# Seven products of a Strassen-Winograd feed-forward in another order, x reloaded in two halves, and modulation sums held back in the mixer

## The chip, the cores and the metric

The kernel runs on one core of a Trainium2 chip. The core has TensorE (PE, whose weight loads the profile lists apart as PEld), VectorE (DVE), ScalarE (ACT), GpSimd (POOL) and SyncE (SP), which here does nothing but issue transfers, in order. The metric is the time of one execution on the device, in microseconds; smaller is better. The kernel before has a median of 1758.36 us over three runs (1758.32 to 1759.86).

## The reference

One layer of an autoregressive trunk on 1024 tokens of width 1024, in float32:

```
x <- x + 1/2 * g1 * SwiGLU_1( adaLN_1(RMSNorm(x)) )
h  = adaLN_2(RMSNorm(x));  [b, c, v, u] = split(h @ W_in)
   yA = b * conv3_causal(c * v)                    (512 channels)
   yB = GLU( Re(C . state) + D*u ),  state_t = Abar state_(t-1) + Bbar u_t   (512 channels)
x <- x + g2 * ( [RMSNorm(yA) | RMSNorm(yB)] @ W_out )
x <- x + 1/2 * g3 * SwiGLU_2( adaLN_3(RMSNorm(x)) )
y  = RMSNorm_final(x)
swiglu(h) = (silu(h @ w_gate) * (h @ w_up)) @ w_down
```

Shift, scale and gate of every sub-layer are columns of silu(cond) @ W_mod + b_mod; they are called the modulation vectors below. The hidden width of a feed-forward is 2816.

## The kernel before, in words

**Arithmetic.** A float32 operand is split into a rounded high part and the rest, and every product is three matmuls: high by high, high by rest, rest by high (`mm3`). So one weight granule has to be loaded, copied to its high part by ACT and subtracted to its rest by VectorE (`Weights.pump`, the groups `w<-raw`). Each call of `mm3` is one tick of a clock that the program keeps while it is written (`Clock.tick`); every `period` ticks the clock takes one step of the side work that is queued, so `clock.period` sets how thinly side work is strewn among the matmuls. The Tile scheduler then sets the final order of each engine's instructions.

**Stages.** The first feed-forward has eleven groups of hidden columns, fa0 to fa10. fa0 to fa3 are plain. From fa4 on each group goes through `seven`: for gate (side g) and then up (side u) the 2 x 2 block product is made of seven products in place of eight, by Winograd's scheme. A product is four calls of `mm3`, twelve matmuls on 128x512. The left blocks A11, A12, A22 and sums S1 to S4 of the normalized activations are made once; the weight blocks' sums t1 to t4 are made for every group by GpSimd (`Weights.combine`, lines L163 and L164; `split_done`, L172 for t2 and L174 for t4). `Weights.SEVEN` is the order in which the weight chunks are prepared: 0, t2, 3, t3, t1, t4, 2. t2 is written over chunk 0 once that is split; t4 = chunk 3 - t2 is written over chunk 3 once that is split, so that both adds stand inside a granule, between what ACT copies.

**Banks of sums.** The list `SEVEN` ahead of `seven` names for each product its left block and its PSUM bank: A11 in A, S2 in B, A12 in A on top of A11, S3 in D, S1 in C, A22 in E, S4 in C. Between them come the additions that take the results out:

```
A.copy(t1[:], bank["A"][:])      # n == 0
add(u2, t1, "B")                 # n == 1
add(u3, u2, "D")                 # n == 3
add(t1, u3, "C")                 # n == 4
add(u3, u3, "E")                 # n == 5
add(u2, u2, "C")                 # n == 6
```

u3 shows in the profile under the name of its tile, fa7gt, fa7gu and so on (a group, a side, a tile). S1's sum has to be out of bank C before S4's first matmul opens it again: in the order before, A22's product is all that stands between. There are six banks for these (`mm_ps`), handed round.

**Around them.** While fa4 to fa9 run, `side1` puts the tables of the S5 state space on VectorE (tiles rot, rott, bb, bl, cl), one step every 7 ticks. The products' results are kept in DRAM (`keep`). `down7` does the down product with the same seven products over chunks of four groups, called fad0 and fad1, each in two passes p = 0 and 1; its left blocks are fetched again (`fetch_chunk`, the names fa1lA, fa1lS) and its weights are raw tiles loaded from in_ds. x, which had to give up its room, is loaded again from DRAM at the start of fa10 by eight transfers of 512 KB (`load_x`).

The mixer follows (w_in, the S5 part, conv, the gated unit `glu`, `w_out`). `side2` makes the modulation vectors of the second feed-forward in it: 24 loads of 512 KB into two buffers (tile wm) and for each a sum on VectorE. In `glu` the root of the norm's mean square is worked out on VectorE by a chain of small operations (nBanv, nBani, nBana, nBany, nBarb), and PE spreads nBarb over the partitions into nBabc. The second feed-forward has the groups fb0 to fb10: fb0 plain, fb1 to fb10 through `seven`, and between fb1's products the down product of fb0, called fb0d (`between` in `seven`, behind the product at position `place`, 0 for fb1).

## Time and profile before

| what | value |
|---|---|
| median of three runs | 1758.36 us |
| the profiled execution | 1760.56 us |
| its span | 1758.8 us |
| PE busy | 1681.3 us, 96% |
| VectorE busy | 1307.3 us, 74% |
| ACT, POOL busy | 569.1 us, 351.2 us |
| mean granted clock of PE | 0.986 |
| read from and written to HBM | 212.47 MB, 86.51 MB |

The span is the stretch from the first to the last instruction that the profiler recorded; the execution's own time has 1.8 us around it. Busy times are by engine and overlap. A row of the waits names who waited for which operation of which engine, for how long in all, how often, and the longest. In a timeline the number in brackets is the idle time of the engine just before, with what ended it.

### The profile page before, as it was taken

Reading aid. Unit: us, or ns where it says so; the run is one execution under the profiler, and the core shown is the slowest. Engines: PE = TensorE matmul, PEld = TensorE weight load, DVE = VectorE, ACT = ScalarE, POOL = GpSimd, SP = SyncE. Lnnn points to the kernel's source line nnn. Section 1 sums busy time; section 2 is a strip of 40 time slices with the busy share of each in tenths; the row PEclk is TensorE's granted clock in tenths of the full one; section 3 lists DMA queues with packets and bytes.
Section 4 is the critical chain, followed back from the end, with each engine's and each line's share of the span. In section 5 each row is a group of like instructions: output and inputs, shape, how many; then the busy total and the mean of one; then the engine's idle time right before and its main releaser. Section 6 shows DMA issues by size and latency. Waiting matters only on the chain.

```text
span 1758.8 us, 20854 instructions
## 1 busy us (share of the span) xinstructions
PE 1681.3 (96%) x7532; PEld 1381.2 (79%) x7532; DVE 1307.3 (74%) x2286; ACT 569.1 (32%) x934; POOL 351.2 (20%) x241
## 2 busy tenths in 40 slices
PE   4999999988999999999999899999999999999996
PEld 3788877876887888878887678878888888888886
DVE  7999899989666687553566876986777666677656
ACT  4223234433332221232213423433344443322221
POOL 0000032232232221100000021023322322333311
PEclk9999999999999999999999999999999999999998
DMA  8245544444677968215664451014344434669312
GB/s 322 80 148 193 203 158 172 171 160 171 230 304 289 355 222 301 88 59 161 191 191 120 149 199 36 25 50 166 132 155 171 166 132 155 226 252 358 120 48 96
DMA packets 101081, 304.55 MB, mean 173 GB/s; under 512 B 19057, under 2 KB 34673, under 8 KB 89842
## 3 DMA queue, kind: packets, MB, share of 16 engines
q1 hardware_dynamic: 100978, 303.22, 47.9%
q8 instruction: 59, 0.97, 0.2%
q14 instruction: 44, 0.36, 0.1%
HBM read 212.47 MB, written 86.51 MB: 170 GB/s over the span
## 4 chain that ended last, share of the span: by engine, by line
PE 63%; DVE 8%; DMA 3%; issue 1%; POOL 1%; ACT 1%; SPq 0%; DVEq 0%; POOLq 0%; ACTq 0%
PE wo L107 4%; PE fald L107 3%; PE fb10d L107 2%; PE u L107 2%; PE fbd_1B L107 2%; PE fbd_0B L107 2%; PE fad_1B L107 2%; DVE w L107 2%; PE fad_0B L107 2%; PE v L107 1%; PE b L107 1%; DMA swz<-si 1%; PE c L107 1%; DVE x L107 1%; PE fb0g L107 1%; PE fbd_1C L107 1%
## 5 line engine op out<-in xcount | busy, mean ns | idle before, releaser
L107 ACT CAST w<-raw 128x512 fp32r<-128x512 f32 (+1 forms) x358 | 237.4, 689 | 527.6 <-POOL raw L172 122.5
L107 DVE TENSOR_TENSOR w<-raw,w 128x512 fp32r<-128x512 f32 (+1 forms) x358 | 303.0, 863 | 136.3 <-ACT w L107 134.9
L172 POOL TENSOR_TENSOR raw<-sums,raw 128x512 f32<-128x512 f32 x50 | 78.0, 1560 | 414.0 <-DVE w L107 387.7
L163 POOL TENSOR_TENSOR sums<-raw 128x512 f32<-128x512 f32 x50 | 69.1, 1382 | 408.6 <-DMA raw<-in_gs 234.1
L174 POOL TENSOR_TENSOR raw<-raw 128x512 f32<-128x512 f32 x50 | 79.8, 1597 | 104.2 <-DVE w L107 95.9
L107 DVE CUSTOM_DVE_ANT_0 wm<-wm,cact 128x1024 f32<-128x1024 f32 x56 | 77.8, 1398 | 14.3 <-DMA wm<-in_wmod 14.2
L164 POOL TENSOR_TENSOR raw<-raw 128x512 f32<-128x512 f32 x50 | 76.5, 1529 | 3.9
L364 POOL TENSOR_TENSOR n3aq<-n3aq,n3aq 128x512 f32<-128x512 f32 x5 | 8.4, 1671 | 283.0 <-DMA wm<-in_wmod 257.4
L107 DVE TENSOR_TENSOR w<-sums,w 128x512 fp32r<-128x512 f32 x50 | 61.7, 1246 | 3.7 <-ACT w L107 3.4
L107 PE MATMUL p<-h,w 128*128 128x512 f32 x192 | 49.6, 421 | 8.1 <-DVE h L107 5.3
L107 PEld LDWEIGHTS p<-h,w 128*128 128x128 f32 x192 | 39.1, 205 | 18.6 <-DVE h L107 6.6
L107 PE MATMUL wo<-oa,w 128*128 128x512 f32 x192 | 45.7, 392 | 1.9 <-ACT w L107 1.2
L107 PE MATMUL v<-h,w 128*128 128x512 f32 x192 | 46.8, 395 | 0.0
L107 PE MATMUL c<-h,w 128*128 128x512 f32 x192 | 46.6, 394 | 0.0
L107 PE MATMUL u<-h,w 128*128 128x512 f32 x192 | 46.3, 401 | 0.2 <-DVE h L107 0.2
L107 PE MATMUL b<-h,w 128*128 128x512 f32 x192 | 45.6, 393 | 0.0
L107 PE MATMUL wo<-ob,w 128*128 128x512 f32 x192 | 45.2, 391 | 0.0
L107 PEld LDWEIGHTS wo<-oa,w 128*128 128x128 f32 x192 | 35.8, 188 | 10.1 <-ACT w L107 1.6
L107 PEld LDWEIGHTS u<-h,w 128*128 128x128 f32 x192 | 36.8, 194 | 8.7 <-DVE h L107 0.6
L107 PEld LDWEIGHTS wo<-ob,w 128*128 128x128 f32 x192 | 35.8, 188 | 7.4
L107 PEld LDWEIGHTS b<-h,w 128*128 128x128 f32 x192 | 35.5, 188 | 7.2
L107 PEld LDWEIGHTS c<-h,w 128*128 128x128 f32 x192 | 35.4, 188 | 7.0
(1565 smaller groups left out, 4042.0 us busy)
## 6 DMA issues: line engine op xcount, KB each, us to landing
raw<-in_gs SPq DMA_DIRECT2D x34, 1024.0 KB, 5.2
wm<-in_wmod SPq DMA_DIRECT2D x56, 512.0 KB, 5.2
raw<-in_ds SPq DMA_DIRECT2D x16, 1024.0 KB, 7.1
raw<-in_gu SPq DMA_DIRECT2D x10, 1024.0 KB, 8.1
mw<-in_wm SPq DMA_DIRECT2D x8, 1024.0 KB, 12.6
x<-in_x SPq DMA_DIRECT2D x16, 512.0 KB, 6.7
raw<-in_win SPq DMA_DIRECT2D x8, 1024.0 KB, 5.6
raw<-in_wl SPq DMA_DIRECT2D x5, 1024.0 KB, 5.5
```

The lines of the kernel that those rows point to most:

```text
L107: r = getattr(self.engine, name)(*args, **kw)
L163: self.G.tensor_tensor(out=f, in0=r[2], in1=r[1], op=ALU.subtract)
L164: self.G.tensor_tensor(out=r[1], in0=r[1], in1=r[0], op=ALU.subtract)
L172: self.G.tensor_tensor(out=r, in0=s["t3"], in1=r, op=ALU.add)
L174: self.G.tensor_tensor(out=r, in0=r, in1=s["t2"], op=ALU.subtract)
L364: nc.gpsimd.tensor_tensor(out=a, in0=a, in1=sq[:, :n], op=ALU.add)
```

## The change

There are three edits.

1. **The order of the seven.** For gate and up the products now go A11, S1, S2, S3, A12, A22, S4, in the banks A, C, B, D, A, E, C. S1's sum is taken out behind S3's, in one go with u3, so that A12's and A22's products stand between it and S4's. The evacuation of A12's bank moves behind the fifth product. The weight chunks go 0, t1, t2, t3, 3, t4, 2; t4 is now written over t2, as soon as that is split, a granule ahead of its use. The tile of the first quarter, c11, comes from another pool where the special one is closed. The down products keep the order of before, as `SECOND`. The callbacks are given a block's name in place of its number. The period of the side work goes from 7 to 7.75.
2. **x in two halves.** At the start of fa10 four of the eight loads are called, the tiles 0 and 2 of both token halves; tiles 1 and 3 are called in the first pass of fad0, behind its third product.
3. **The mixer's sums.** The period for side2 goes from 10 to 8 ahead of the gated unit, is 1000 from there until five tasks of the output product have been called, and 3 after them (before, it was 5 behind the second half of the gated unit).

How the instructions move is seen in the order in which the engines hold them. TensorE in the middle of fa7's gate side, before (fa7gC is bank C of group fa7, side g; h1S are the activations' sums, h_1 the second token half; x3 are the three matmuls of a split product):

```order
L107 MATMUL fa7gC<-h1S_3_1670,w_3259 128x512 x3
L107 MATMUL fa7gE<-h_1_419,w_3259 128x512 x3
L107 MATMUL fa7gE<-h_1_458,w_3259 128x512 x3
L107 MATMUL fa7gE<-h_1_497,w_3259 128x512 x3
L107 MATMUL fa7gE<-h_1_531,w_3259 128x512 x3
L107 MATMUL fa7gC<-h1S_0_2073,w_3314 128x512 x3
```

and with the change:

```order
L107 MATMUL fa7gD<-h1S_3_1708,w_3161 128x512 x3
L107 MATMUL fa7gA<-h_0_416,w_3225 128x512 x3
L107 MATMUL fa7gA<-h_0_455,w_3225 128x512 x3
L107 MATMUL fa7gA<-h_0_494,w_3225 128x512 x3
L107 MATMUL fa7gA<-h_0_528,w_3225 128x512 x3
L107 MATMUL fa7gE<-h_1_419,w_3225 128x512 x3
L107 MATMUL fa7gE<-h_1_458,w_3225 128x512 x3
L107 MATMUL fa7gE<-h_1_497,w_3225 128x512 x3
L107 MATMUL fa7gE<-h_1_531,w_3225 128x512 x3
L107 MATMUL fa7gC<-h1S_0_2073,w_3263 128x512 x3
```

The four rows of fa7gE alone stood between the two uses of fa7gC; now the rows of fa7gA stand ahead of them too, and the first use of C lies further up, behind A11's rows.

SP around the end of fa10, before (kept10A is a result of fa10 that goes to DRAM and waits for it; raw are the weights of the second pass of fad0):

```order
L107 DMA fa1lS_4638<-kept1S_545 128x1024
L107 DMA kept10A_600<-fa10A_4627 128x1024
L107 DMA fa2lS_4640<-kept2S_552 128x1024
L107 DMA fa3lS_4642<-kept3S_559 128x1024
L107 DMA fa4lS_4644<-kept4S_566 128x1024
L107 DMA raw_4780<-in_ds 128x2048
L107 DMA raw_4812<-in_ds 128x2048
```

and with the change:

```order
L107 DMA kept10A_600<-fa10A_4625 128x1024
L107 DMA fa1lS_4634<-kept1S_545 128x1024
L107 DMA fa2lS_4636<-kept2S_552 128x1024
L107 DMA fa3lS_4638<-kept3S_559 128x1024
L107 DMA fa4lS_4640<-kept4S_566 128x1024
L107 DMA x_1_4306<-in_x 128x1024
L107 DMA raw_4780<-in_ds 128x2048
L107 DMA raw_4812<-in_ds 128x2048
```

The fetch fa1lS went from ahead of kept10A to behind it, and the last load of x stands ahead of the two raw loads; seven others of x go earlier, as all eight did.

VectorE in the gated unit, before (wm ... scl is a sum of side2, into the scale):

```order
L107 ISA wm_3_0_7957,scl<-wm_3_0_7957,cact_7580 128x1024
L107 ISA scl 128x1
L107 TENSOR_SCALAR nBani<-nBani 128x4
L107 TENSOR_TENSOR nBana<-nBani 128x4
L107 SCALAR_TENSOR_TENSOR nBana<-nBana,nBanv 128x4
L107 ISA wm_3_1_7996,scl<-wm_3_1_7996,cact_7580 128x1024
L107 ISA scl 128x1
L107 SCALAR_TENSOR_TENSOR nBany<-nBana,nBani 128x4
L107 TENSOR_TENSOR scl<-scl,cols 128x8
L107 TENSOR_TENSOR nBana<-nBany 128x4
L107 SCALAR_TENSOR_TENSOR scl<-scl,cols 128x8
L107 SCALAR_TENSOR_TENSOR nBana<-nBana,nBanv 128x4
```

and with the change, up to nBarb:

```order
L107 SCALAR_TENSOR_TENSOR nBana<-nBana,nBanv 128x4
L107 SCALAR_TENSOR_TENSOR nBany<-nBana,nBani 128x4
L107 TENSOR_TENSOR nBana<-nBany 128x4
L107 SCALAR_TENSOR_TENSOR nBana<-nBana,nBanv 128x4
L107 SCALAR_TENSOR_TENSOR nBany<-nBana,nBany 128x4
L107 TENSOR_TENSOR nBana<-nBany 128x4
L107 SCALAR_TENSOR_TENSOR nBana<-nBana,nBanv 128x4
L107 ISA wm_3_0_8289,scl<-wm_3_0_8289,cact_7580 128x1024
L107 ISA scl 128x1
L107 SCALAR_TENSOR_TENSOR nBany<-nBana,nBany 128x4
L107 COPY nBarb<-nBany 128x512
L107 TENSOR_TENSOR yb_7573<-yb_7573,gs_1_8018 128x512
```

The scheduler has put other sums at this place: before, wm_3_0 and wm_3_1 stood between nBani and nBarb, and wm_2_0 and wm_2_1 ahead of nBanv; now it is wm_2_0 and wm_2_1 (a few rows further up) and wm_3_0, and wm_3_1 stands behind.

The diff:

```diff
--- before.py
+++ after.py
 class Weights:
-    SEVEN = (0, "t2", 3, "t3", "t1", "t4", 2)
+    SEVEN = (0, "t1", "t2", "t3", 3, "t4", 2)
+    SECOND = (0, "t2", 3, "t3", "t1", "t4", 2)
     def __init__(self, engines, srcs, granules, raw_bufs):
...
         self.G.tensor_tensor(out=r[1], in0=r[1], in1=r[0], op=ALU.subtract)
-        self.sums[j] = {"t1": r[1], "t2": r[0], "t3": f, "t4": r[3]}
+        self.sums[j] = {"t1": r[1], "t2": r[0], "t3": f, "t4": r[0]}
     def split_done(self, j, c):
-        if j in self.combined and c in (0, 3):
-            s, r = self.sums[j], self.chunk(j, c)
+        if j in self.combined and c in (0, "t2"):
+            s, r = self.sums[j], self.raws[j][:, :HALF]
             if c == 0:
...
             else:
-                self.G.tensor_tensor(out=r, in0=r, in1=s["t2"], op=ALU.subtract)
+                self.G.tensor_tensor(out=r, in0=self.chunk(j, 3), in1=r, op=ALU.subtract)
     def chunk(self, j, c):
...
                 srcs.extend([ds[c, p, 0], ds[c, p, 1]])
-                granules.extend([(j, s), (j + 1, s)] for s in Weights.SEVEN)
+                granules.extend([(j, s), (j + 1, s)] for s in Weights.SECOND)
         plain([wl[i] for i in range(wl.shape[0])])
...
                     x[2 * k + i][h] = xt[k][h][:, i, :]
-    def load_x(h):
-        for k in range(KT // 2):
-            SP.dma_start(xt[k][h][:], x_d[h, :, 2 * k : 2 * k + 2, :])
+    def load_x(hs, ks=range(KT // 2)):
+        for h in hs:
+            for k in ks:
+                SP.dma_start(xt[k][h][:], x_d[h, :, 2 * k : 2 * k + 2, :])
     def mm3(out, w, k, act, first, last, tok=slice(0, HALF), more=False):
...
             yield
-    SEVEN = (("A11", "A"), ("S2", "B"), ("A12", "A"), ("S3", "D"), ("S1", "C"), ("A22", "E"), ("S4", "C"))
+    SEVEN = (("A11", "A"), ("S1", "C"), ("S2", "B"), ("S3", "D"), ("A12", "A"), ("A22", "E"), ("S4", "C"))
+    SECOND = (("A11", "A"), ("S2", "B"), ("A12", "A"), ("S3", "B"), ("S1", "C"), ("A22", "B"), ("S4", "C"))
     def seven(name, between, place=1, kept=None, then=None):
...
                     A.copy(t1[:], bank["A"][:])
-                elif n == 1:
+                elif n == 2:
                     u2 = t2k(nm + "u2")
                     add(u2, t1, "B")
-                elif n == 2 and side == "g":
-                    t = pools["first"].tile([P, HALF], F32, tag="first", name=nm + "c11") if "first" in pools else t2k(nm + "c11")
+                elif n == 3:
+                    u3 = t2k(nm + "u3")
+                    add(u3, u2, "D")
+                    add(t1, u3, "C")
+                    out(1, 1, t1)
+                elif n == 4 and side == "g":
+                    t = pools["first"].tile([P, HALF], F32, tag="first", name=nm + "c11") if "first" in pools else acc_in_mov(nm + "c11")
                     A.activation(t[:], bank["A"][:], AF.Silu)
                     gate_[0, 0] = t
-                elif n == 2:
+                elif n == 4:
                     t = gate_[0, 0]
...
                         keep(kept, "A11", t, name)
-                elif n == 3:
-                    u3 = t2k(nm + "u3")
-                    add(u3, u2, "D")
-                elif n == 4:
-                    add(t1, u3, "C")
-                    out(1, 1, t1)
                 elif n == 5:
...
                         keep_sums(kept, gate_[0, 0], u3, t1, name)
-                else:
+                elif n == 6:
                     add(u2, u2, "C")
...
                 if side == "u" and then is not None:
-                    then(n)
+                    then(left)
         return a_tiles
...
         return t[:, 0, :], t[:, 1, :]
-    def down7(name, lefts, n_, then=None):
+    def down7(name, lefts, n_, then=None, first=None):
         for p in range(2):
...
                 V.tensor_tensor(out=dst[i][:], in0=src[i][:], in1=bank[b, i][:], op=ALU.add)
-            for n, (left, b) in enumerate(SEVEN):
+            for n, (left, b) in enumerate(SECOND):
                 (w,) = ws.take()
-                b = "B" if b in "DE" else b
                 for i in range(2):
...
                 ws.free()
-                if p and then is not None:
-                    then(n)
+                if (first, then)[p] is not None:
+                    (first, then)[p](left)
     def down2(a_tiles, n, name, halves=(1, 0)):
...
     mod_load(0)
-    load_x(0)
-    load_x(1)
+    load_x(range(2))
     ws.load(1)
...
         gate_up(act1, f"fa{g}", kept[g], g == SEVEN_FROM[0] - 1)
-    clock.period = 7
+    clock.period = 7.75
     lefts = [{left: [] for left, _ in SEVEN} for _ in range(CHUNKS)]
...
     HOMES = dict(A11="A", S2="B", A12="A", S3="B", S1="B", A22="A", S4="A")
-    def fetch_chunk(c, n, name="fa"):
-        left = SEVEN[n][0]
+    def fetch_chunk(c, left, name="fa"):
         for g in range(1 + 4 * c, 5 + 4 * c):
             lefts[c][left].append(fetch(kept[g], left, HOMES[left], f"{name}{g}l"))
-    def fetch_last(n):
-        if n in (0, 2, 5):
-            i = (0, 2, 5).index(n)
+    def fetch_last(left):
+        if left in ("A11", "A12", "A22"):
+            i = ("A11", "A12", "A22").index(left)
             for h in range(2):
...
             open_x(ctx)
-            for h in range(2):
-                load_x(h)
+            load_x(range(2), (0, 2))
         if g == NGRP - 2:
             pools.pop("first")
-        seven(f"fa{g}", lambda: None, kept=kept[g], then=(lambda n: fetch_chunk(0, n)) if g == NGRP - 1 else None)
-    down7("fad0", lefts[0], 0, lambda n: fetch_chunk(1, n))
+        seven(f"fa{g}", lambda: None, kept=kept[g], then=(lambda left: fetch_chunk(0, left)) if g == NGRP - 1 else None)
+    down7("fad0", lefts[0], 0, lambda left: fetch_chunk(1, left), lambda left: load_x(range(2), (1, 3)) if left == "A12" else None)
     clock.period = 8
...
     SP.dma_start(pools["cact"][:], cact_d[:])
-    clock.period = 10
+    clock.period = 8
     clock.side.append(side2(lambda name: wmp.tile([P, 1024], F32, tag="wm", name=name, bufs=2)[:], (SC3, SH3, G3)))
...
             n3[h].add(x[d][h], beside=d < 6)
+    clock.period = 1000
     wgl = ws.take(2)
...
     glu(1)
-    clock.period = 5
     ws.free(2)
...
     w_out((0, 1), 1, 1)
+    clock.period = 3
     ws.free(2)
...
     a_last = {}
-    def fetch_last(n):
-        if n == 0:
+    def fetch_last(left):
+        if left == "A11":
             for h in range(2):
...
         seven(f"fb{g}", lambda: None, kept=kept[g])
-    a_prev = seven("fb10", lambda: None, then=lambda n: fetch_chunk(0, n, "fb"))
-    down7("fbd0", lefts[0], 2, lambda n: fetch_chunk(1, n, "fb"))
+    a_prev = seven("fb10", lambda: None, then=lambda left: fetch_chunk(0, left, "fb"))
+    down7("fbd0", lefts[0], 2, lambda left: fetch_chunk(1, left, "fb"))
     down7("fbd1", lefts[1], 2, fetch_last)
```

## The prediction

> **What bounds the kernel now.** I read the head of the page first. The groups of costly instructions name VectorE and ACT, but the share of the span belongs to TensorE:
>
> ```profile
> span 1758.8 us, 20854 instructions
> PE 1681.3 (96%) x7532; PEld 1381.2 (79%) x7532; DVE 1307.3 (74%) x2286; ACT 569.1 (32%) x934; POOL 351.2 (20%) x241
> ```
>
> PE is idle for 1758.8 − 1681.3 = 77.5 us in all, prologue and tail included. The change takes no matmul away, so it can win only idle time of PE and time at a low clock. Next, the windows over the stage that the new order touches most, the first feed-forward's groups fa4 to fa9 (columns: stretch, its length, busy us of PE, PEld, DVE, ACT and POOL with counts, granted clock, DMA share, GB/s):
>
> ```profile
> 240.00:280.00 40.00, 36.88 (x160) 29.41 (x159) 39.02 (x64) 14.82 (x26) 9.23 (x7) 0.96 0.50 175
> 280.00:320.00 40.00, 38.25 (x174) 31.08 (x173) 36.98 (x58) 16.44 (x29) 11.50 (x8) 1.00 0.44 164
> 320.00:360.00 40.00, 39.74 (x181) 32.28 (x181) 37.28 (x62) 15.31 (x27) 11.97 (x8) 1.00 0.44 163
> 360.00:400.00 40.00, 34.71 (x149) 27.32 (x147) 33.12 (x50) 12.98 (x23) 12.78 (x8) 0.96 0.40 132
> 400.00:440.00 40.00, 34.63 (x150) 27.37 (x150) 36.14 (x58) 13.62 (x25) 13.16 (x8) 0.96 0.48 175
> 440.00:480.00 40.00, 40.00 (x175) 32.59 (x174) 25.52 (x42) 16.06 (x28) 10.20 (x8) 0.95 0.61 221
> sum 240.00, PE 224.21 PEld 180.06 DVE 208.06 ACT 89.23 POOL 68.83; mean PE 37.37 PEld 30.01 DVE 34.68 ACT 14.87 POOL 11.47
> 235.60:436.90 201.30, 186.36 (x822) 149.27 (x821) 181.97 (x287) 74.32 (x131) 60.73 (x38) 0.98 0.46 164
> ```
>
> PE lacks 240 − 224.2 = 15.8 us here. What the clock withholds is 40 × (0.04 + 0 + 0 + 0.04 + 0.04 + 0.05) = 6.8 us. So **22.6 us are in play**. While the side work on the S5 tables runs, VectorE is the fuller engine; in 440–480, without it, PE lacks nothing. The waits of PE, VectorE and ACT in 240–480 (total, times, longest, us) name the hand-over:
>
> ```profile
> PE fa7gC L107 <- DVE fa7gt L107: 4.6, 1, 4.6
> PE fa8uC L107 <- DVE fa8ut L107: 3.8, 1, 3.8
> PE fa4uC L107 <- DVE fa4ut L107: 2.4, 1, 2.4
> PE fa5gC L107 <- DVE fa5gt L107: 1.8, 1, 1.8
> PE fa8uA L107 <- ACT fa8ut L107: 1.1, 1, 1.1
> DVE w L107 <- ACT w L107: 17.6, 11, 3.2
> ACT w L107 <- POOL raw L172: 22.2, 8, 4.6
> ```
>
> Bank C holds S1's product, VectorE adds it out, and S4's product opens C again. The timeline of fa7g shows it, with E's product the only cover between:
>
> ```profile
> 358.83 2.85 POOL L172 TENSOR_TENSOR raw<-sums,raw 128x512 f32<-128x512 f32 x1 [14.81 <-DVE w L107]
> 360.90 2.88 PE L107 MATMUL fa7gE<-h,w 128*128 128x512 f32 x12
> 361.72 1.14 ACT L107 CAST w<-raw 128x512 fp32r<-128x512 f32 x2 [4.26 <-POOL raw L172]
> 364.19 1.75 DVE L107 TENSOR_TENSOR rot<-rs,rt 128x512 f32<-128x512 f32 x1
> 368.34 4.57 PE L107 MATMUL fa7gC<-h1S,w 128*128 128x512 f32 x12 [4.56 <-DVE fa7gt L107]
> 371.01 0.68 DVE L107 TENSOR_TENSOR rot<-rs,rt 128x512 f32<-128x512 f32 x1
> 458.77 2.72 PE fa9gE L107 x12
> ```
>
> The last row is from the chain of waits: twelve matmuls of one product take 2.72 us when nothing holds them. The twelve after the stall took 4.57 us, at a clock that had dropped.
>
> **Edit 1, the seven products.** Between S1's sum out of C and S4's product there is one product now, 2.72 us; afterwards there are two (A12, A22), 5.44. A12 waits for A11's copy behind three products, not one, so the 1.1-us kind of wait goes. VectorE must keep pace too. The busy time per instruction in fa4u to fa8u is 181.97 / 287 = 0.634 us. I counted VectorE's instructions in the two orders between successive last C sums, side by side (4u, 5g, … 8u): before 30, 37, 22, 38, 21, 42, 29, 32, 35; after 28, 28, 32, 27, 31, 39, 20, 39, 21. The sum goes from 286 to 265, or 182 to 168 us, because the period of 7.75 pushes side work into fa9: 9g goes from 28 to 40 and 9u from 13 to 21. PE itself needs about 201.3 − 15 of stalls − 4 of clock = 182 us for these nine, so VectorE falls below PE in the sum; the peaks remain. One side is 7 × 2.72 = 19.0 us of PE. At 7g VectorE needs 39 × 0.634 = 24.7, an excess of 5.7, and 6u before it (31 × 0.634 = 19.7) leaves 0.6 more; the cover is 5.44 − 0.69 for the sum itself = 4.75. So 7g still stalls 0.6 + 5.7 − 4.75 = 1.5, 8g 0.9 and 9g (25.4) 1.6: 4.0 us, and I add 1 for one half-length low-clock stretch. The term is 5 − 22.6 = **−17.6**. Bounds: −22.6 (all vanishes) and −6 (VectorE stays the bound, below).
>
> The clock deserves a look: a gap of 2.44 us in fa4u, and the clock behind it (the same columns as above):
>
> ```profile
> 259.41 4.57 PE L107 MATMUL fa4uC<-h1S,w 128*128 128x512 f32 x12 [2.44 <-DVE fa4ut L107]
> 260.00:264.00 4.00, 4.00 (x13) 3.14 (x12) 3.96 (x5) 0.62 (x1) 1.62 (x1) 0.63 0.17 66
> ```
>
> The 2.44-us gap brought 0.63. [...]
>
> **Edit 1's weights.** t2 and t4 are made a granule earlier, so ACT no longer queues behind POOL within a granule: the 22.2 us of ACT and, through it, much of VectorE's 17.6. The POOL adds then run beside a VectorE that works. The rows speak of a price: `rot` took 1.75 us beside POOL's 2.85-us add and 0.68 alone. [...] The result that this gives is the second rival. The same POOL and ACT instructions run either way; −17.6 holds their move at nothing, covered by VectorE's 182 − 168 = 14 us of new room.
>
> **Edit 2, x in two halves.** Of the eight 512-KB loads, the first four stay where all eight were, at the start of fa10, and three of the rest still go early. On SP's in-order queue the fourth, and the fetch fa1lS, which stood ahead of kept10A, now stand behind kept10A and ahead of the two raw loads for down7's second half. These rows show that place:
>
> ```profile
> 545.71 0.32 SPq L107 DMA_DIRECT2D kept10A<-fa10A  x1
> 547.89 0.87 SPq L107 DMA_DIRECT2D raw<-in_ds  x2
> 553.00:557.00 4.00, 4.00 (x20) 3.30 (x19) 1.71 (x3) 0.39 (x1) 0.36 (x1) 1.00 1.02 430
> 556.64 1.29 POOL L163 TENSOR_TENSOR sums<-raw 128x512 f32<-128x512 f32 x1 [28.93 <-DMA raw<-in_ds]
> PE fad_0A L107 <- DVE w L107: 3.2, 3, 1.9
> 566.00:570.00 4.00, 3.80 (x10) 3.00 (x11) 2.18 (x3) 0.99 (x2) 3.92 (x3) 0.59 0.03 12
> ```
>
> POOL waits for the raws, and PE, behind POOL, ACT and VectorE, already stalls 3.2 us; nothing covers more. Two more transfers of 0.52 MB at 430 GB/s are **+2.4 us**. Bounds: −4.8 (the stall, and 4 × 0.41 = 1.6 of clock, go because x leaves the link early) and +4.5 (twice the delay less an overlap of its issue). The first half of x: nothing, under fa10's matmuls.
>
> **Edit 3, the gated unit.** These rows carry it, the last showing the length of one sum:
>
> ```profile
> PE nBabc L107 <- DVE nBarb L107: 4.9, 1, 4.9
> 988.00:1020.00 32.00, 27.09 (x125) 22.47 (x123) 29.02 (x68) 13.03 (x20) 2.34 (x1) 0.95 0.47 161
> 993.38 1.22 DVE L107 CUSTOM_DVE_ANT_0 wm<-wm,cact 128x1024 f32<-128x1024 f32 x1
> ```
>
> The period of 1000 lets no new sum start there, yet in the new order the scheduler still leaves three in VectorE's chain up to nBarb: the count ahead of it falls by one only, 1.22 us, and wm_3_0 now needs a load that can go only after wm_2_0 is added. I take **−0.5**, bounds −6.5 (4.9 and 32 × 0.05 of clock) and +2. The sums held back follow in w_out, where VectorE has room until 1100; I take 0, ±1.
>
> **Edit 1 in the second feed-forward.** From fb2 on VectorE has no side work, and nothing changes. At fb1, A12 was second, and PE used it between fb0's down products:
>
> ```profile
> 1160.22 1.98 PE L107 MATMUL fb1gA<-h,w 128*128 128x512 f32 x8
> PE fb0d L107 <- DVE x L107: 1.7, 3, 0.7
> ```
>
> In the new order nothing stands there: 0 to +2.7 (one product), and I take **+1.5**.
>
> **The sum** is −17.6 + 2.4 − 0.5 + 1.5 = −14.2. The profiled execution took 1760.6 (1758.8 in its span and 1.8 around it), 2.2 above the median of the runs, 1758.36. So 1746.4 for such an execution and **1744.2** for the median.
>
> **Rivals.**
> 1. *All cover holds.* E's and A12's products hide every peak (−22.6), the raws come no later (0), and the chain in the gated unit empties (−4.9): 1758.4 − 27.5 + 1.5 = 1732. For it: the waits outside 7g and 8u are 2.4 us and less, under the new 2.72 of cover. Against it: three peaks of 39 and 40 instructions.
> 2. *VectorE stays the bound.* POOL's adds, which ran in VectorE's 17.6 idle us, now block it: while they overlap it does 0.68 / 1.75 = 0.39 of its work, so 17.6 × 0.61 = 10.7 us more. With all of its 19.3 idle us kept it needs 168 + 10.7 + 19.3 = 198 of 201.3 (−3.3); with half, 188 (−13). Midway −8, and with the other terms −4.6: 1754. For it: the `rot` rows. Against it: PE stood still in 360–440 while VectorE was idle too, so its room was unused.
> 3. *Slower, by bank B.* Bank C is now second in a side and B third, so if banks go round in turn the next side's S2 takes the bank that S4's sum has to free: two products after S4, 5.44 us, where it was five, 13.6. Should VectorE come over 4.75 us late to S4's sum, PE waits in every side; at 6.4 late (two weight chunks behind ACT's 3.2) it is (6.4 + 0.69 − 5.44) × 12 = 20 us: 1764. Against it, this sum in fa4u started 1.6 us after S4's last product (259.41 + 4.57 = 263.98), and in fb1g it waited for PE:
>
> ```profile
> 265.46 0.68 DVE L107 TENSOR_TENSOR fa4uu<-fa4uu,fa4uC 128x512 f32<-128x512 f32 x1
> 1180.80 0.69 DVE L107 TENSOR_TENSOR fb1gu<-fb1gu,fb1gC 128x512 f32<-128x512 f32 x1 [0.36 <-PE fb1gC L107]
> ```
> 4. *The change doesn't do what it says, the other way round:* I hold that the sums stay in the gated unit. If they do leave it, the 4.9-us wait goes, not 0.5: 1740.
>
> **How the numbers follow.** Forecast 0.56, by itself 1738 to 1750 (term 1 by ±4, the rest by ±2). Rival 1: 0.12; rival 2: 0.2; rival 3: 0.06; rival 4: 0.06. The measurement can tell about 0.2%, 3.5 us, from no change. Faster: 0.56 + 0.12 + 0.06 and half of rival 2's 0.2, 0.84; same: the other half, 0.1; slower 0.06. The range 1733 to 1756 leaves out rival 3, the lower half of rival 1 and the ends of 2 and of the forecast, about 0.18.
>
> **What would show it.** Right: PE's waits on fa4 to fa8 sums at some 4 us, all in front of 7g, 8g and 9g; ACT's wait for POOL under 5 us; clock 0.99 and more in these windows; fad_0A's wait at 5 to 6; nBabc's at 4 to 5; fb0d's waits up. Wrong: fa-B banks waiting for a u2 sum (rival 3), VectorE over 95% busy in 240–440 with PE waiting at every side (rival 2), or waits that show up at fa10 or in w_out.

## The result, and the profile after

The changed kernel takes **1748.95 us** (median of 4 runs, 1747.75 to 1752.1) against 1758.62 for the kernel before beside it: a ratio of 0.9946, interval 0.9929 to 0.9964, so 9.5 us or 0.54% faster. The forecast was 1744.2, the range 1733 to 1756. The direction and the range held; the gain is two thirds of the forecast one.

The head of the page of the profiled execution after:

```profile
span 1750.3 us, 20808 instructions
PE 1677.9 (96%) x7532; PEld 1379.6 (79%) x7532; DVE 1300.6 (74%) x2286; ACT 566.0 (32%) x934; POOL 351.1 (20%) x241
```

The span is 8.5 us shorter. To see where, I cut both spans at the same events, the first matmul of a product, and compared the pieces (starts from the view of each tile; PE's idle time is a piece's length less PE's busy time in the view of windows):

| piece | before, us | after, us | difference | PE idle before, after |
|---|---|---|---|---|
| start to fa4g | 218.7 | 219.2 | +0.5 | 25.8, 26.0 |
| fa4g to fa9g | 224.3 | 206.7 | −17.6 | 15.8, 4.7 |
| fa9g to fad_0A | 78.2 | 79.3 | +1.1 | 0.0, 1.2 |
| fad_0A to the projection u | 225.7 | 230.7 | +5.0 | 3.5, 5.6 |
| u to the gated unit (gl) | 209.8 | 210.1 | +0.3 | 5.5, 6.9 |
| gl to fb0d | 181.1 | 178.3 | −2.8 | 10.8, 8.8 |
| fb0d to fb2g | 61.8 | 66.9 | +5.1 | 2.8, 6.1 |
| fb2g to the end | 559.2 | 559.1 | −0.1 | 13.3, 13.1 |

The first feed-forward won 16.5 us up to the down product, nearly what was forecast (17.6). The down product and fb1 gave back 10.1, where the sum held 3.9. The windows of fa4 to fa8 and of fb0d to fb2, first before, then after:

```profile
218.70:443.00 224.30, 208.51 (x913) 166.85 (x912) 204.81 (x324) 84.24 (x149) 65.86 (x41) 0.97 0.46 164
1137.80:1199.60 61.80, 59.00 (x253) 46.73 (x252) 51.27 (x76) 19.93 (x35) 17.11 (x11) 1.00 0.16 60
```

```profile
219.20:425.90 206.70, 202.03 (x913) 164.72 (x912) 194.77 (x303) 82.47 (x148) 64.62 (x41) 0.99 0.48 172
1124.30:1191.20 66.90, 60.81 (x254) 47.73 (x253) 51.52 (x76) 19.64 (x35) 18.80 (x11) 0.97 0.18 63
```

PE has the same matmuls in both. In the first piece VectorE has 10 us less to do (204.8 to 194.8, 21 instructions fewer), and the time that it is not busy falls from 19.5 to 11.9 us. In the second it has the same work, and PE idles more. The waits after, that answer to those of the prediction (VectorE's and ACT's are those of the stretch 240 to 480, as there):

```profile
PE fa7gC L107 <- DVE fa7gt L107: 2.6, 1, 2.6
PE fa5uC L107 <- DVE fa5ut L107: 2.1, 1, 2.1
PE fa9gC L107 <- DVE fa9gt L107: 1.2, 1, 1.2
PE fad_0A L107 <- DVE w L107: 2.8, 2, 1.7
PE fad_0B L107 <- ACT w L107: 1.8, 1, 1.8
PE nBabc L107 <- DVE nBarb L107: 3.9, 1, 3.9
PE fb0d L107 <- DVE x L107: 5.1, 4, 2.0
DVE w L107 <- ACT w L107: 5.7, 6, 3.1
ACT w L107 <- POOL raw L173: 14.2, 7, 4.4
```

Bank C's waits went from 13.6 us in the list before (7g, 8u, 4u, 5g, 7u, 6g) to 5.9 in three, and the waits of A12 for A11's copy are gone. VectorE's wait for ACT fell from 17.6 to 5.7, ACT's for GpSimd only from 22.2 to 14.2. The stall at 5u is in a side with 32 VectorE instructions, well below the 39 and 40 that the count named. The trace points to its cause, which no run tried alone: just ahead of its sums GpSimd's adds for the weights run beside VectorE's table work, and two operations on `rot` tiles take 1.78 us each, where the same two took 0.69 at 287.68 and 289.00, with no add beside them.

```profile
291.76 1.61 POOL L173 TENSOR_TENSOR raw<-sums,raw 128x512 f32<-128x512 f32 x1 [10.20 <-DVE w L107]
293.33 1.74 POOL L164 TENSOR_TENSOR sums<-raw 128x512 f32<-128x512 f32 x1
292.13 1.78 DVE L107 TENSOR_TENSOR rot<-rs,rt 128x512 f32<-128x512 f32 x1
293.84 1.78 DVE L107 TENSOR_TENSOR rott<-rs,rt 128x512 f32<-128x512 f32 x1
```

These two rows alone are 2.2 us too long, and PE's stall there is 2.1. fad_0B's wait is new. fb0d's wait for x went from 1.7 to 5.1; PE's timeline there, after:

```profile
1141.28 3.02 PE L107 MATMUL fb0d<-fb_0a,w 128*128 128x512 f32 x12 [2.01 <-DVE x L107]
1145.01 1.67 PE L107 MATMUL fb0d<-fb_0a,w 128*128 128x512 f32 x6 [0.70 <-DVE x L107]
1149.94 6.04 PE L107 MATMUL fb0d<-fb_1a,w 128*128 128x512 f32 x18 [1.87 <-DVE x L107]
```

Eighteen matmuls took 6.04 us at a granted clock of 0.72; in the kernel before, eighteen of fb0d (from 1146.99 on) took 4.37 at 1.00. So the clock dropped here too: 3.4 us of longer waits and 1.7 of clock make the 5.1. Such a place is called a half-clock stretch below: in the one at 557.90 of the changed kernel's down product three matmuls took 1.28 us until the next three started, in the rows around it 0.68.

### The profile page after: what moved, and what is told of

Same layout as the page of the kernel before. It is cut to its first block, busy times and chain, and to the rows that moved or that the text cites. A ratio compares the mean times of both kernels' runs of the same rounds, so it can differ in the third digit from the quotient of the medians.

```text
span 1750.3 us, 20808 instructions
## 1 busy us (share of the span) xinstructions
PE 1677.9 (96%) x7532; PEld 1379.6 (79%) x7532; DVE 1300.6 (74%) x2286; ACT 566.0 (32%) x934; POOL 351.1 (20%) x241
## 4 chain that ended last, share of the span: by engine, by line
PE 76%; DVE 14%; DMA 5%; issue 2%; POOL 1%; ACT 1%; SPq 1%; DVEq 0%; POOLq 0%; ACTq 0%
PE wo L107 4%; PE fald L107 3%; DVE w L107 3%; PE p L107 2%; PE fb10d L107 2%; PE fbd_0B L107 2%; PE fbd_1B L107 2%; PE u L107 2%; DMA swz<-si 2%; PE b L107 1%; DVE x L107 1%; PE c L107 1%; PE fa3u L107 1%; PE fb0g L107 1%; PE fa2g L107 1%
## 5 line engine op out<-in xcount | busy, mean ns | idle before, releaser
L107 DVE TENSOR_TENSOR w<-raw,w 128x512 fp32r<-128x512 f32 (+1 forms) x358 | 295.9, 845 | 107.3 <-ACT w L107 106.5
L164 POOL TENSOR_TENSOR sums<-raw 128x512 f32<-128x512 f32 x50 | 71.4, 1429 | 451.5 <-DMA raw<-in_gs 263.3
L175 POOL TENSOR_TENSOR raw<-raw 128x512 f32<-128x512 f32 x50 | 77.5, 1549 | 89.6 <-DVE w L107 73.0
L165 POOL TENSOR_TENSOR raw<-raw 128x512 f32<-128x512 f32 x50 | 77.3, 1547 | 3.2
L107 DVE TENSOR_TENSOR w<-sums,w 128x512 fp32r<-128x512 f32 x50 | 52.5, 1063 | 3.6 <-ACT w L107 3.0
```

Of the source, the lines that this page charges most:

```text
L107: r = getattr(self.engine, name)(*args, **kw)
L164: self.G.tensor_tensor(out=f, in0=r[2], in1=r[1], op=ALU.subtract)
L165: self.G.tensor_tensor(out=r[1], in0=r[1], in1=r[0], op=ALU.subtract)
L175: self.G.tensor_tensor(out=r, in0=self.chunk(j, 3), in1=r, op=ALU.subtract)
```

## The experiments

All ratios are to the kernel before, run beside each on the same chip; the changed kernel's own is 0.9946 (0.9929 to 0.9964). One profile catches one execution, and these strayed up to some 3 us from their kernel's median. So a small difference of a single piece is a weak sign, unless several kernels that share its code agree.

**x loaded whole.** Edit 2 undone.

```diff
-            load_x(range(2), (0, 2))
+            load_x(range(2))
-    down7("fad0", ..., lambda left: load_x(range(2), (1, 3)) if left == "A12" else None)
+    down7("fad0", ...)
```

> The changed kernel with edit 2 undone: all eight loads of x are issued at the start of fa10 again, nothing else differs. Theory (the raw loads of the second pass of fad0 come late because one load of x and the fetch fa1lS now stand ahead of them on SP; landing measured from kept10A went from 10.9 to 13.4 us): the raws land about 1.2 to 2.4 us earlier, the stretch from fad_0A's first product to fald shrinks from 162.6 us towards the 158.6 of the kernel before, and the whole run is 2 to 4 us faster than the changed kernel's 1749. Rival (the late raws come from the new order of the fetches, not from x): the stretch stays at 162 to 163, and the total within 1 us of 1749. Second rival (loading all of x at fa10 delays the fetches and the weights there): fa10 or the first pass of fad0 gets a new wait, and the total is 1 to 3 us above 1749.

Measured: 1750.41 us, ratio 0.9963 (0.9951 to 0.9975): no faster than the change, and by the ratios 0.2% slower, inside the intervals. PE's idle time between fad_0A and u is 5.4 us against 5.6. The raws did land sooner behind kept10A, 12.1 us against 13.4 with the change (kept10A at 529.73, the add at 543.10) and 10.9 before, as the timeline of SP and GpSimd shows:

```profile
530.26 0.32 SPq L107 DMA_DIRECT2D kept10A<-fa10A  x1
542.34 1.41 POOL L164 TENSOR_TENSOR sums<-raw 128x512 f32<-128x512 f32 x1 [34.35 <-DMA raw<-in_ds]
```

PE's waits stayed all the same: 3.2 us on fad_0A (2.8 with the change) and 1.8 on fad_0B. The theory that x's last load makes the down product wait falls: 1.3 us of landing bought nothing. The fetch fa1lS still stands behind kept10A here. In the run with the period of 7 below, it and all of x go ahead of kept10A; the raws land 10.3 us behind it (537.00 to 547.28), sooner than before the change, and PE still waits 4.1 us on fad_0A. So this delay as a whole is not what PE waits for. The second rival, that loading all of x early costs 1 to 3 us, isn't told from zero.

**t4 of the down weights at its old place.** Edit 1 made t4 early for all combined weights, the down products' too.

```diff
+        self.late = {j for pair in granules if pair[0][1] == pair[1][1] for j, _ in pair}
-        ... "t4": r[0]}
+        ... "t4": r[3] if j in self.late else r[0]}
...
-        if j in self.combined and c in (0, "t2"):
+        if j in self.late and c == 3:
+            self.G.tensor_tensor(out=self.chunk(j, 3), in0=self.chunk(j, 3), in1=self.sums[j]["t2"], op=ALU.subtract)
+        elif j in self.combined and (c == 0 or c == "t2" and j not in self.late):
```

> The changed kernel with t4 of the down products' weights alone made where it was before, over chunk 3 behind its split; gate and up keep the new place. Theory (with the new place GpSimd makes t4 of the first raw tile ahead of the two adds of the second, which now run a granule later: from the first add of fad0's second pass to the second tile's t2 it is 11.5 us in the changed kernel and 10.6 before; this is the 1.8-us wait of fad_0B for ACT that no run with the old place shows): that wait goes, PE's idle time from fad_0A to the projection u falls from 5.6 to about 3.8 us, the total by 1.8 us, or 3.5 where a half-clock stretch goes with it. Rival (the second raw tile is late by its transfer, whatever GpSimd does first): the wait stays within 0.5 us, and the total too.

Measured: 1748.0 us, ratio 0.9946 (0.9934 to 0.9958): the total doesn't tell it from the change. The profile does show the step. GpSimd's timeline after, where t4 (L175) stands ahead of the second tile's adds (L164, L165), and then with the old place, where t4 (L172) stands behind them:

```profile
549.48 1.67 POOL L175 TENSOR_TENSOR raw<-raw 128x512 f32<-128x512 f32 x1 [1.45 <-DVE w L107]
551.10 1.73 POOL L164 TENSOR_TENSOR sums<-raw 128x512 f32<-128x512 f32 x1
552.91 1.62 POOL L165 TENSOR_TENSOR raw<-raw 128x512 f32<-128x512 f32 x1
```

```profile
546.93 1.29 POOL L165 TENSOR_TENSOR sums<-raw 128x512 f32<-128x512 f32 x1
548.30 1.62 POOL L166 TENSOR_TENSOR raw<-raw 128x512 f32<-128x512 f32 x1
550.54 1.67 POOL L172 TENSOR_TENSOR raw<-raw 128x512 f32<-128x512 f32 x1 [0.63 <-DVE w L107]
```

and the wait of PE that answers to the new one:

```profile
PE fad_0B L107 <- ACT w L107: 0.5, 1, 0.5
```

fad_0B's wait fell from 1.8 to 0.5 (and 0.5 more for VectorE), PE's idle time in the piece from 5.6 to 4.4. Other kernels agree: the wait is 1.8 in six profiles with t4 early (the change, x loaded whole, and four of the runs below), and 0.5 again in the one with both losses mended. With the periods of 7 and 9 it is absent though t4 is early: with 7 one of the second tile's adds runs ahead of t4, with 9 PE waits longer elsewhere. Of the new wait in the down product this is the cause; it is worth about 1 us, less than a whole run shows.

**Another order in fb1 alone.** A12's product, which needs no sum from VectorE, stands second again.

```diff
+    INNER = (0, 3, "t1", "t2", "t3", "t4", 2)                       # the weights of fb1
...
+    INNER = (("A11", "A"), ("A12", "A"), ("S1", "C"), ("S2", "B"), ("S3", "D"), ("A22", "E"), ("S4", "C"))
...
-    seven("fb1", lambda: down2(a_prev, 2, "fb0", (0, 1)), 0, kept[1])
+    seven("fb1", lambda: down2(a_prev, 2, "fb0", (0, 1)), 0, kept[1], order=INNER)
```

> The changed kernel with another order of products in fb1 alone: A11, A12, S1, S2, S3, A22, S4, with the weights in the order 0, 3, t1, t2, t3, t4, 2, so that A12's product, which needs no sum of VectorE's, is at hand again between fb0d's products. Theory (the 5.0 us lost between fb0d's first product and fb1's second product are A12's absence as a filler: 3.4 us more of waits for x and 1.6 of clock): fb0d's waits for x fall from 5.1 to 1.5 to 2.5 us, and the total falls by 4 to 5 us, to about 1744 to 1745. Rival (VectorE, full with the sums of the normalized activations and the updates of x, is the bound there, so that a filler only moves the stall behind itself): the waits move to fb1's S1 or stay, and the total falls by less than 1.5 us.

Measured: 1744.9 us, ratio 0.9932 (0.992 to 0.9943). The wait of fb0d, and the window of the piece:

```profile
PE fb0d L107 <- DVE x L107: 2.4, 2, 1.5
```

```profile
1121.50:1183.10 61.60, 58.58 (x254) 46.86 (x253) 50.97 (x76) 19.81 (x35) 16.48 (x11) 1.00 0.17 60
```

The piece is back at 61.6 us (66.9 with the change, 61.8 before), its clock at 1.00. VectorE's busy time is the same 51 us in all three, and it has no idle time in 1137 to 1152 with the change, where PE waits. So the missing filler is the cause of the 5 us; the rival, a bound by VectorE that no filler helps, falls.

**The mixer's periods of before.** Edit 3 undone.

```diff
-    clock.period = 8
+    clock.period = 10
...
-    clock.period = 1000
...
     glu(1)
+    clock.period = 5
...
-    clock.period = 3
```

> The changed kernel with edit 3 undone: the period of the modulation sums is 10 ahead of the gated unit, not 1000 in it, and 5 behind its second half. Theory (the 2.5 us gained between the projection u and the second feed-forward come from edit 3): nBabc's wait returns from 3.9 to about 4.9 us, the wait of the output product for ACT from 0.2 to 1.2, and the total rises by 1.5 to 3 us to about 1751. Rival (the scheduler leaves the sums where they are, and the gain comes from the changed lead of the stages before): the total stays within 1 us.

Measured: 1749.55 us, ratio 0.9958 (0.9945 to 0.9971): 0.1% above the change, inside the intervals. nBabc's wait returned:

```profile
PE nBabc L107 <- DVE nBarb L107: 4.9, 1, 4.9
```

PE's idle time from gl to fb0d is 11.0 us here, 10.8 in the kernel before, and 8.7 to 10.0 in the kernels that keep edit 3, all of which have nBabc's wait at 3.9. So the edit takes 1 to 2 us of idle time out of the gated unit; the totals agree in sign and can't show it alone.

**The period of 7 again.**

```diff
-    clock.period = 7.75
+    clock.period = 7
```

> The changed kernel with the side work of the first feed-forward every 7 ticks again. Counted in VectorE's order, no side then has more than 35 instructions between last bank-C sums (4u to 9u: 25, 33, 23, 33, 32, 30, 31, 35, 27, 23, 15) against peaks of 39 at 7g and 8g and 40 at 9g with 7.75. Theory of the prediction (each side has 19.0 us of PE and a cover of 4.75, at 0.634 us an instruction): the peaks of 33 to 35 are 20.9 to 22.2 us, which the cover takes one at a time, but 6g, 6u, 7g, 7u, 8g stand in a row with 161 instructions, 102 us against 95 of PE, 7 over a cover of 4.75, so 2 to 3 us of stalls late, near 8g, instead of the 5.9 with 7.75: total 1 to 4 us lower than 1749. Rival (VectorE's total is what counts, 286 or more instructions are the stage's bound): stalls of 8 us and more from 6u on, total 3 to 6 us above 1749.

Measured: 1756.95 us, ratio 1.0003 (0.9993 to 1.0013). The whole gain is gone, where I had expected one to four us more. So I turned it round.

**The kernel before, with the period of 7.75 alone.**

```diff
-    clock.period = 7
+    clock.period = 7.75
```

> The kernel before with one number changed: the side work of the first feed-forward every 7.75 ticks, not 7. Theory V (VectorE bounds fa4 to fa8: from fa4g's first product to fa9g's the stretch is VectorE's busy time plus what it idles, 204.8 + 19.5 = 224.3 us before, 194.8 + 11.9 = 206.7 with the whole change, 204.0 + 12.1 = 216.1 with the change at period 7; so the period takes 9 to 10 us of work out of it, and the order takes 7.5 of idle time): the stretch falls to 213 to 216 us, the total by 8 to 10 us to about 0.995 of the kernel before. Rival S (what counts is the cover in bank C, one product here; the peaks of side work stay as stalls): the stretch stays above 220 and the total falls by less than 4 us.

Measured: 1756.89 us, ratio 1.0002 (0.9992 to 1.0011). In the time of the whole run neither the order without the period nor the period without the order is worth anything that can be measured; together they bring 0.54%. The windows of the two pieces, fa4g to fa9g and fa9g to fad_0A, first with the change and period 7, then with the kernel before and period 7.75:

```profile
218.60:434.70 216.10, 203.32 (x913) 164.35 (x912) 203.99 (x319) 81.51 (x148) 63.94 (x41) 0.98 0.48 169
434.70:512.50 77.80, 77.80 (x350) 64.11 (x349) 50.43 (x73) 30.12 (x53) 24.49 (x17) 1.00 0.70 266
```

```profile
218.60:434.10 215.50, 205.51 (x914) 165.35 (x913) 196.07 (x310) 84.54 (x149) 63.46 (x41) 0.98 0.46 165
434.10:517.10 83.00, 78.96 (x350) 63.80 (x349) 59.61 (x87) 29.65 (x52) 24.36 (x16) 1.00 0.68 249
```

The first piece splits cleanly. Length less VectorE's busy time is 19.5 us before, 19.4 with the period alone, 12.1 with the order alone, 11.9 with both; the busy time is 204.8 and 204.0 at a period of 7, 196.1 and 194.8 at 7.75. The period takes work out, the order takes time in which VectorE stands, and in this piece the two add up: 8.8, 8.2 and 17.6 us. In the next piece they don't: the pushed-out work costs PE 4.0 us of idle time with the old order, 1.2 with the new one. Theory V is right on the first piece (213 to 216 expected, 215.5 found) and wrong on the total, where rival S's number came true. By the profiles the order alone gains 8.6 us up to fad_0A and gives 6.0 back in the down product and in fb1 (pieces of 227.9 and 65.6 us, against 225.7 and 61.8 before). Whether the remaining 2.6 are there the timed runs, whose interval is 1.8 us to either side, don't say: the profile of period 7 lay 1.5 us below its kernel's median, that of the kernel before 2.2 above.

**t2 in the granule of chunk 0 again.** Two products of cover remain, ACT waits for GpSimd within the granule.

```diff
-    SEVEN = (0, "t1", "t2", "t3", 3, "t4", 2)
+    SEVEN = (0, "t2", "t1", "t3", 3, "t4", 2)
...
-    SEVEN = (("A11", "A"), ("S1", "C"), ("S2", "B"), ("S3", "D"), ...
+    SEVEN = (("A11", "A"), ("S2", "B"), ("S1", "C"), ("S3", "D"), ...
...
```

The rest of the edit makes `seven` ask for a block's name in place of its number.

> The changed kernel with S2 ahead of S1 in gate and up, and so with the weight chunk t2 in the same granule as chunk 0, as before: ACT waits for GpSimd's add within the granule again. S1's sum still stands behind S3's, with two products of cover to S4, t4 is still made early, the period is 7.75. Theory W (the idle time that the order took from VectorE was its wait for ACT behind GpSimd, 17.6 us before and 5.7 after; the second product of cover adds little): VectorE's wait for ACT in fa4 to fa9 returns to 12 us or more, the stretch from fa4g to fa9g rises from 206.7 to 212 to 215, the total by 5 to 8 us to about 1755. Rival S (the cover in bank C is what won the time): the wait of ACT returns, VectorE catches up within the cover, and the total stays within 2 us of the changed kernel.

Measured: 1758.49 us, ratio 1.001 (1.0001 to 1.002). The waits of VectorE and ACT, and the windows of the two pieces:

```profile
DVE w L107 <- ACT w L107: 14.6, 9, 2.5
ACT w L107 <- POOL raw L173: 38.8, 11, 5.2
```

```profile
218.70:428.00 209.30, 202.90 (x914) 164.51 (x913) 192.03 (x303) 82.74 (x148) 57.87 (x40) 0.99 0.47 167
428.00:513.30 85.30, 79.71 (x349) 65.02 (x348) 61.19 (x92) 30.65 (x55) 22.58 (x17) 0.98 0.67 251
```

Over this stretch, 218 to 445, VectorE's wait for ACT is back at 14.6 us (12.5 before, 2.0 with the change), and the whole gain is gone, as theory W says. The place is not the one it named: the first piece lost 2.6 us, the next one 6.0, with waits of 3.3 us in fa9g and 2.2 in fa9u.

**One product of cover, t2 a granule later.**

```diff
-    SEVEN = (0, "t1", "t2", "t3", 3, "t4", 2)
+    SEVEN = (0, "t3", "t2", 3, "t1", "t4", 2)
...
-    SEVEN = (("A11", "A"), ("S1", "C"), ("S2", "B"), ("S3", "D"), ("A12", "A"), ("A22", "E"), ("S4", "C"))
+    SEVEN = (("A11", "A"), ("S3", "D"), ("S2", "B"), ("A12", "A"), ("S1", "C"), ("A22", "E"), ("S4", "C"))
...
```

u3's sum is now taken out behind S2's product, and S1's alone behind its own.

> The changed kernel with the products of gate and up in the order A11, S3, S2, A12, S1, A22, S4 and the weight chunks 0, t3, t2, 3, t1, t4, 2: the chunk t2 stands a granule behind chunk 0, as in the change, so that ACT needs not wait for GpSimd, but between S1's sum and S4's product there is one product again, as in the kernel before. Period 7.75. Theory W (in fa4 to fa8 the length is VectorE's busy time plus its idle time; the weights' order took 7.5 us of idle time, and the second product of cover does nothing there): VectorE's idle time in that stretch stays at 11 to 13 us, and the stretch at 206 to 209, the total within 3 us of the changed kernel. Theory S (the cover is what counts): stalls of bank C of 8 us and more return, the stretch rises to 212 and above, the total by 5 us or more. Both agree that fa9, where the side work that was pushed out now runs, may lose up to 4 us with one product of cover.

Measured: 1755.83 us, ratio 0.999 (0.9981 to 0.9999). The waits of PE and VectorE, and the window of fa4 to fa8:

```profile
PE fa7gC L107 <- DVE fa7gt L107: 3.6, 1, 3.6
PE fa5uC L107 <- DVE fa5ut L107: 3.1, 1, 3.1
DVE w L107 <- ACT w L107: 4.3, 4, 2.4
```

```profile
217.30:433.00 215.70, 205.94 (x914) 166.23 (x913) 200.11 (x306) 82.43 (x148) 59.93 (x41) 0.98 0.46 165
```

VectorE's wait for ACT stays low (4.3, and 5.5 in 240 to 480, where the change has 5.7), and yet the piece is 215.7 us, with 9.8 of PE's idle time in place of 4.7. So theory W's other half falls. That the cover alone does it is not shown, since this order also lengthened VectorE's work: 200.1 us for 306 instructions, 5.3 more than with the change. The by-form view puts that into the weights: 72 subtractions took 57.9 us here and 52.3 with the change. Why these are longer stays open.

**The period of 9.**

```diff
-    clock.period = 7.75
+    clock.period = 9
```

> The changed kernel with the side work of the first feed-forward every 9 ticks. Theory V (VectorE bounds fa4 to fa8): in VectorE's order 15 instructions fewer stand between the last bank-C sums of fa4g and fa8u, about 9 us of work; PE's idle time of 4.7 us in the stretch falls below 1.5 and its 1.7 of half clock goes, the stretch falls from 206.7 to 201 to 203 us, and the total by 3 to 5 us to about 1744 to 1745. Rival (the work that is pushed out is missing further on: the tables of the S5 part come late, or fa9 and fa10 with 23 instructions on the gate side get the stalls): as much is lost in fa9 and fa10 or in the projections, and the total stays within 1.5 us of the changed kernel.

Measured: 1765.51 us, ratio 1.0048 (1.0036 to 1.0061), the slowest of all. Theory V is right where it looked and irrelevant: the first piece falls to 204.2 us, VectorE's busy time to 186.5. The pieces behind it lose far more, as their windows, SP's timeline around the start of fa10 and PE's waits show:

```profile
421.80:509.50 87.70, 82.88 (x362) 67.24 (x361) 69.65 (x105) 31.26 (x56) 25.90 (x18) 0.96 0.59 220
509.50:749.90 240.40, 228.32 (x977) 185.23 (x976) 157.45 (x226) 53.42 (x87) 53.18 (x34) 0.96 0.69 255
```

```profile
479.25 4.76 SPq L107 DMA_DIRECT2D mk_d<-kc  x8
486.60 1.98 SPq L107 DMA_DIRECT2D x<-in_x  x4
```

```profile
PE fad_0A L107 <- ACT w L107: 4.8, 1, 4.8
PE fad_0C L107 <- DMA fa1lS<-kept1S: 2.8, 1, 2.8
```

The side work is not done when fa10 starts (465.2 us here), its last tables (mk_d) go out at 479, and x follows at 486.6, 21 us into fa10. With the change the last tables go out at 458.3 and the first load of x at 470.4, 3.3 us into fa10. SP issued the fetches for the down product behind them (fa3lA to fa4lS 31.0 to 33.8 us into fa10, 14.1 to 25.8 with the change), four loads of x even behind kept10A, and the down product waits for them: 12.1 us of PE's idle time against 5.6. That is one half of the loss. The other, 8.4 us in fa9 and fa10, comes ahead of it: PE waits 2.9 us for VectorE's table bl and 1.9 for a sum of fa9g, and the clock is 0.96.

**Both losses mended**, fb1's order and the down weights' t4, the diffs of above together.

> The changed kernel with two of its losses mended at once: the order A11, A12, S1, ... in fb1 alone, and t4 of the down products' weights at its old place. Expected, if the two are separate: fb0d to fb2 5 us shorter, as in the run with the first alone, and PE's idle time from fad_0A to u at 4.4 us; a total of 0.992 to 0.993 of the kernel before, 1743 to 1744 us. If they were the same loss seen twice, no more than the first alone gave, 0.9932.

Measured: **1743.26 us**, ratio **0.9913** (0.9899 to 0.9927), the fastest kernel of this study, 0.33 points below the change. The profile has both mended, the windows from fad_0A to u and from fb0d to fb2:

```profile
504.40:732.50 228.10, 223.26 (x977) 182.50 (x976) 162.50 (x228) 53.24 (x87) 52.56 (x34) 0.99 0.70 258
1120.60:1182.20 61.60, 58.55 (x253) 46.85 (x252) 50.96 (x76) 19.80 (x35) 16.44 (x11) 1.00 0.17 60
```

PE's idle time from fad_0A to u is 4.8 us, where the run with fb1's order alone has 6.7. So the two losses lie in separate places. By the time alone t4's share is not shown: 0.9913 and 0.9932 have intervals that overlap.

**The same with a period of 8.**

```diff
-    clock.period = 7.75
+    clock.period = 8
```

> The kernel with both mended, and a period of 8 in the first feed-forward. The periods 7 and 9 cost 8 and 17 us against 7.75, 7 since VectorE has 9 us more to do in fa4 to fa8, 9 since the side work is not done by the end of fa9 and the rest, put out in one piece at the start of fa10, makes the raw loads of the down products late. With 8 the side work still ends in fa9 (15 instructions a side in fa10, as with 7.75, against 23 with 9). If these two are the reasons, 8 gains up to 2 us in fa4 to fa8 and loses none at fa10: within 2 us of the same kernel at 7.75, rather below. If the time depends on where single side jobs fall among the sums, it can be up to 5 us longer.

Measured: 1746.24 us, ratio 0.9933 (0.9919 to 0.9946): 0.2% above the run with 7.75, in intervals that overlap, and the two profiled executions took the same (1744.14 and 1744.08). So it is not faster; that it is slower is not shown. The first piece did gain 1.9 us (204.8), the down product lost them again (6.5 us of idle time against 4.8). SP's timeline shows a likely reason, and that the side work did not end in fa9 as I had expected:

```profile
467.49 3.12 SPq L107 DMA_DIRECT2D mk_d<-kc  x5
530.01 2.34 SPq L107 DMA_DIRECT2D x<-in_x  x4
```

fa10 starts at 463.8; with 7.75 the last tables are out before it (462.9, fa10 at 466.3). Here four loads of x go behind kept10A and ahead of the raws, which land 15.3 us behind it in place of 13.0, and PE waits 5.4 us on fad_0A for ACT. With the period of 9 the same happened in a larger size.

## Why the prediction was right, and where it was wrong

The sum forecast −14.2 us and the runs gave −9.5. The direction and the size of the largest term came from the mechanism that was named. The nearness of the total owes something to luck as well: terms 2 and 4 were too small by 6.2 us together, and term 3 gave back 2.3, part of it a half-clock stretch that no step of the sum had.

- **Term 1, the seven products: −17.6 forecast, −16.5 measured** (fa4g to fad_0A). The mechanism is the one named, VectorE late to bank C, and the residual stalls of 4.0 us at 7g, 8g and 9g came as 5.9 at 7g, 5u and 9g. The count of 39 and 40 instructions found two places of three; the third, 5u, it could not find, since it took every instruction at the mean of 0.634 us, and there, beside GpSimd's adds, single ones took 1.78. The single half-clock stretch that was added came, at fa7g (0.58 over 4 us); the 1 us taken for it was an estimate that no run shows, it cost 1.7.
- **Edit 1's weights.** "−17.6 holds their move at nothing" was wrong as a reading. Undoing this move takes the whole gain away (1.001), as does going back to one product of cover (0.999, with the reservation above) or to the period of 7 (1.0003). None of the three is a spare. That ACT "no longer queues behind POOL" came in part only: its wait fell to 14.2 us, where the sign was under 5.
- **Term 2, x in halves: +2.4 forecast, +5.0 measured, and the step named was the wrong one.** The raws landed 2.4 us later behind kept10A, as worked out from 0.52 MB at 430 GB/s. But fad_0A's wait, which was to rise to 5 or 6 us, fell from 3.2 to 2.8; loading x whole took 1.3 us of the delay away and none of the waits, and with period 7 there is no delay and PE waits no less (4.1). A larger delay may count: with four loads in that place (the periods of 8 and 9) PE waits 5.4 and 6.5 us for ACT. What showed a cause of its own is edit 1's early t4 in the down weights, a part that the sum priced at nothing: 1.2 of the 2.1 us of additional idle time. Another 1.7 us are a second half-clock stretch (a clock of 0.87 and 0.70 in 544 to 552 and of 0.65 and 0.92 in 556 to 564, 1.7 us each; before, 0.84 and 0.73 in 564 to 572 alone); the rest is not assigned. Two other profiles of the same code (fb1's order, the mixer's periods) took 229.2 and 229.7 us for the piece in place of 230.7.
- **Term 3, the gated unit: −0.5 forecast, −2.8 measured.** nBarb's wait fell by 1.0 us. In the kernels that keep edit 3 the piece's idle time is 1 to 2 us lower, so the edit was under-sized by about 1; PE's busy time is 0.8 us lower in this profile, with one half-clock stretch fewer (by windows of 4 us the clock withheld 5.2 us in 960 to 1004 before, 3.4 in 952 to 988 after). The output product's wait for ACT went from 1.2 to 0.2 here, but is 1.2 to 1.4 in four other runs that keep the edit, so it is not the edit's. The sums did not leave the unit, as the order of the instructions said, and rival 4 did not come.
- **Term 4, fb1: +1.5 forecast with a bound of +2.7, measured +5.1.** This is the failed size. The bound priced the missing filler at the length of one product. But the gap belongs to VectorE, which is full there with the sums and the updates of x (15.0 of the 15 us from 1137 on): without a filler PE waits for x four times, 5.1 us in place of 1.7, and behind these waits came a half-clock stretch (0.72 over 6.04 us, 1.7 lost). The run with the filler back gives both back.
- **Rival 1** (all cover holds) did not come: 5.9 us of stalls stayed. **Rival 2** (VectorE stays the bound) came in part: in fa4 to fa8 the length is still VectorE's busy time and 12 us more, in the changed kernel as in that with period 7. Its price, GpSimd's adds that stretch VectorE's work, is seen at 5u (1.78 us in place of 0.69). In the kernel before, the 1.75-us `rot` row at 364.19 ran beside adds of 1.58 and 1.67 us; beside the 2.85-us add from 358.83 on, three operations of VectorE took their usual 0.68, so 0.39 did not hold for every overlap. In all the price is not 10.7 us: VectorE's mean instruction went from 0.632 to 0.643 us, some 3 us over 303 of them. The mean hides two moves, and the instructions are not all the same in the two: the three forms of `rot` took 0.12 to 0.23 us more each (31 of them, 5 us), and the weights' subtractions 5.5 us less in all. That fits adds which moved from beside the weights to beside the tables; no run tried it. **Rival 3** (bank B) left no trace: no wait of a bank B for a sum of u2 stands among the waits of gate and up.

Totals hide what these runs did in the stage itself. The same cuts as above, by one profile each:

| kernel | fa4g to fad_0A, us | fad_0A to the end, us |
|---|---|---|
| before | 302.5 | 1237.6 |
| before, period 7.75 alone | 298.5 | 1238.0 |
| the change with period 7 | 293.9 | 1240.7 |
| the change with t2 behind chunk 0 | 294.6 | 1243.4 |
| the change with one product of cover | 295.2 | 1241.5 |
| the change | 286.0 | 1245.1 |
| the change, both losses mended | 285.7 | 1237.8 |

Six kernels that share the code of the first stage with the change took 285.5 to 286.0 us for it. Any two of the three parts win some 7 to 9 us there, about half of the 16.5. (The kernel before has a single profile here, 2.2 us above its median, so these gains may be up to that much smaller.) The four kernels with the new order and neither loss mended are 3 to 8 us longer than the kernel before behind that stage, by losses in the down product and in fb1, and so the totals of those with two parts show nothing. The cover alone and the weights' move alone were not run.

## What to carry to other kernels

Where an engine off the bound is nearly as full as the bound (here VectorE, 194.8 of 206.7 us, and PE, 202.0), a hand-over can need several things at once: cover on the waiting engine, a chain without a wait on the late engine, and room in its work. Here any two of the three won about half of what all three won in that stage, and by the time of the whole run nothing, since the same order lost as much further on. So compare the stages before an edit is thrown away for its total, and look for what it costs elsewhere. When products are put in another order, look for the place where one of them served as a filler between the work of a fuller engine: the gap is that engine's, not the filler's length, and here it cost 1.7 us of slow clock on top. And work that is pushed later has a date: past the start of what its engine or its queue had to do next, it cost more here than the stalls that it relieved.
